# Rows of a mixture of experts: four quarter gathers and square-block transposes on VectorE in place of one gather and TensorE transposes

## The chip, the cores and the metric

The kernel runs on one core of one Trainium2 chip. The metric is the device time of one execution in microseconds (us); less is better. TensorE (PE) multiplies matrices into PSUM, VectorE (DVE), ScalarE (ACT) and GpSimd (POOL) work on elements, and SyncE (SP) and POOL issue the transfers (DMA) between HBM and SBUF. An engine takes its instructions in the order in which the program has them in that engine's queue.

## The reference, cut to what matters

One layer of a decoder for 512 prompt tokens, 64 sample tokens and 16 meta tokens of width 1024: attention and gated linear attention, and then a mixture of experts for the 576 tokens that are returned. Only the last part is touched:

```python
def hier_moe(h, w_group, b_group, w_er, b_er, w_g, w_u, w_d):
    hf = h.reshape(n * l, d)                       # RMSNorm of the residual stream, d = 1024
    ...                                            # top-1 group of 4, then top-2 of its 8 experts
    gates = jnp.sum(jax.nn.one_hot(e_id, N_EXPERTS, dtype=F32) * w_sel[..., None], axis=1)
    y = jnp.zeros_like(hf)
    for e in range(N_EXPERTS):                     # 32
        he = jax.nn.silu(hf @ w_g[e]) * (hf @ w_u[e])   # 1024 -> 256, twice
        y = y + gates[:, e:e + 1] * (he @ w_d[e])       # 256 -> 1024
    return y.reshape(n, l, d)
```

## The kernel before, in words

The last third of the program is the mixture of experts. `out_proj` ends the mixer; while its last quarter of columns is multiplied, `route_tile(i)` runs for each of five tiles of 128 tokens. It transposes the residual rows, computes the router's logits, scales the rows and writes them to `h2d` in HBM (L1217, L1218), and finds each token's two experts and its place among that expert's tokens. `table_tile` adds the tile to a table: a comparison on DVE (`pc`, L1278) and a product on PE (L1281) per choice. `tables` then makes from it, for 16 pairs of experts with 64 slots each, so 128 slots a pair, the row number `ix`, the token `tk` and the `gate` of each slot.

`moe` walks over the 16 pairs (`ep`). For a pair, `gather_x` fetches the 128 slots' rows into one of three tiles `xg` (an indirect DMA on POOL's queue, three pairs ahead), and `slots_t` turns them into `xt`, eight blocks of 128 features by 128 slots: eight transposes on PE into PSUM (L1340), then four copies by ACT and one by DVE that scale by `gk` (L1342, L1346). `pair_up` multiplies `xt` by the gate and up weights into `pj` (with the transposes of the pair before, `prod_t`, in its middle), ACT and DVE make `th` (L1359 to L1361). `pair_down` multiplies the pair before by its down weights into `dn`; ACT and DVE split the result into a high and a low half, `yh` (L1385) and `yl` (L1386). After every second pair `add_back` sends two pairs' results back to the tokens' rows: ten groups of four products `ab` on PE, each added to `x2` by DVE (L1400); two PSUM buffers hold the groups (`psA`).

In a round of the loop the order on every engine is the order of the code, since `mm`, `tr` and the marked DVE instructions are kept in program order: `pair_up(ep)`, `down(ep - 1)`, `slots_t` of pair ep + 1, and in every second round `back()`. Below, a round with `back()` is a long round (seven in the loop, plus the last `back` behind it), one without it a short round (pair ep + 1 prepared with no `ab` behind). The weights come through SP's queue into rings of buffers; those of experts 4 and 5 wait for small copies on POOL (L1309).

Of the kernel before, what the change touches and what calls it, by code (L numbers as in the profile page):

```python
# [11 lines left out]
F32 = mybir.dt.float32  # L12
F32R = mybir.dt.float32r
I32 = mybir.dt.int32
# [12 lines left out]
NQ = NP_ + NS  # L27
# [38 lines left out]
class Kern:  # L66
# [1086 lines left out]
    def route(self, rp):  # L1153
        nc, A, c = self.nc, self.A, self.rcp
        wr = rp.tile([128, 8, 36], F32, name="wr")
        nc.sync.dma_start(wr[:, :, 0:4], A["w_group_router"][0].rearrange("(k p) n -> p k n", p=128))
        nc.sync.dma_start(wr[:, :, 4:36], A["w_expert_router"][0].rearrange("(k p) n -> p k n", p=128))
        self.gk = c.tile([128, 8], F32, name="gk")
        nc.sync.dma_start(self.gk, A["norm_ffn_g"].rearrange("o (p k) -> p (o k)", p=128))
        gk = rp.tile([128, 8], F32, name="gkr")  # L1160
        nc.sync.dma_start(gk, A["norm_ffn_g"].rearrange("o (k p) -> p (o k)", p=128), allow_slow_non_contiguous=True)
        nc.gpsimd.tensor_tensor(wr, wr, gk[:, :, None].to_broadcast([128, 8, 36]), op=OP.mult)
        br = rp.tile([128, 36], F32, name="br")
        nc.sync.dma_start(br[:, 0:4], A["b_group_router"].to_broadcast([128, 4]))
        nc.sync.dma_start(br[:, 4:36], A["b_expert_router"].to_broadcast([128, 32]))
        self.i640 = c.tile([128, 640], F32, name="i640")
        nc.gpsimd.iota(self.i640, pattern=[[1, 640]], base=0, channel_multiplier=0, allow_small_or_imprecise_dtypes=True)
        i64 = c.tile([128, 64], F32, name="i64")
        nc.gpsimd.iota(i64, pattern=[[1, 64]], base=0, channel_multiplier=0, allow_small_or_imprecise_dtypes=True)
        tri = rp.tile([128, 128], BF16, name="tri")  # L1170
        ob = rp.tile([128, 128], BF16, name="ob")
        tf = rp.tile([128, 128], F32, name="trif")
        nc.gpsimd.memset(tf, 1.0)
        nc.gpsimd.affine_select(tf, tf, pattern=[[1, 128]], compare_op=OP.is_gt, fill=0.0, base=0, channel_multiplier=-1)
        nc.vector.tensor_copy(tri, tf)
        nc.vector.memset(ob, 1.0)
        iu = self.iu = rp.tile([128, 32], U32, name="iu")
        nc.vector.tensor_copy(iu, i64[:, 0:32])
        oh = c.tile([128, 5, 2, 32], BF16, name="oh")
        nc.gpsimd.memset(oh, 0.0)  # L1180

        val = c.tile([128, 5, 2, 2], F32, name="val")
        nc.gpsimd.memset(val[:, 4, :, 1], 0.0)
        for r in range(2):
            nc.gpsimd.iota(val[:, :, r, 0], pattern=[[128, 5]], base=-int(FAR), channel_multiplier=1, allow_small_or_imprecise_dtypes=True)
        pos = c.tile([128, 5, 2], F32, name="pos")
        self.oh, self.val, self.pos, self.i64 = oh, val, pos, i64
        self.rt = (rp, wr, br, tri, ob)
        self.tps = self.S2()[:, 0]

    def route_tile(self, i):
# [22 lines left out]
        lg = t(36, "lg")  # L1214
        nc.vector.scalar_tensor_tensor(lg[:w], ps[:w, 0:36], ss[:w], br[:w], op0=OP.mult, op1=OP.add)

        nc.scalar.activation(h2[:w].rearrange("t (k p) -> t p k", k=8), x.rearrange("t (p k) -> t p k", k=8), AF.Copy, scale=ss[:w])  # L1217
        nc.sync.dma_start(self.h2d[i * 128:i * 128 + w, :], h2[:w])  # L1218
        g8 = t(8, "g8")
        nc.gpsimd.memset(g8, NEG)  # L1220
# [52 lines left out]
    def table_tile(self, tp, ps, i):  # L1273

        nc = self.nc
        for r in range(2):
            pc = tp.tile([128, 2, 64], F32, name="pc", bufs=2)
            nc.vector.tensor_scalar(pc, self.i64[:, None, :].to_broadcast([128, 2, 64]), self.pos[:, i, r:r + 1], None, op0=OP.is_equal)  # L1278
            ov = tp.tile([128, 2, 32], F32, name="ov", bufs=2)
            nc.gpsimd.tensor_tensor(ov, self.oh[:, i, r, None, :].to_broadcast([128, 2, 32]), self.val[:, i, r, :, None].to_broadcast([128, 2, 32]), op=OP.mult)  # L1280
            nc.tensor.matmul(ps[:, 0:64], lhsT=pc.rearrange("p a b -> p (a b)"), rhs=ov.rearrange("p a b -> p (a b)"),  # L1281
                             start=(i == 0 and r == 0), stop=(i == 4 and r == 1))

    def tables(self, tp, c, ps):

        nc = self.nc
        psv = ps[:, 0:64].rearrange("p (a b e) -> p a b e", a=2, e=2)
        ix = c.tile([128, 16], I32, name="ix")
        tk = c.tile([128, 16], F32, name="tk")
        gate = c.tile([128, 16], F32, name="gate")  # L1290
        hs = [slice(64 * e, 64 * e + 64) for e in range(2)]
        for e, q in enumerate(hs):
            nc.vector.tensor_scalar(ix[q], psv[q, 0, :, e], FAR, None, op0=OP.add)
        for e, q in enumerate(hs):
            nc.vector.tensor_scalar(tk[q], psv[q, 0, :, e], FAR, None, op0=OP.add)
            nc.vector.tensor_scalar(gate[q], psv[q, 1, :, e], 0.5, None, op0=OP.mult)
        return tk, gate, ix


    def gather_x(self, xg, col):  # L1300
        self.nc.gpsimd.indirect_dma_start(xg, None, self.h2d[:, :], bass.IndirectOffsetOnAxis(ap=col, axis=0),  # L1301
                                          bounds_check=NQ - 1, oob_is_err=False)

    def load_up(self, pool, e, behind=None):

# [27 lines left out]
    def slots_t(self, xg, mp):  # L1333

        nc = self.nc
        xt = mp.tile([128, 8, 128], F32, name="xt")
        for q in range(2):
            ps = self.tp_()
            for k in range(4):
                self.tr(ps[:, k * 128:(k + 1) * 128], xg[:, (4 * q + k) * 128:(4 * q + k + 1) * 128], self.ident)  # L1340
            if q:
                nc.vector.tensor_tensor(xt[:, 4:8], ps.rearrange("p (k t) -> p k t", t=128),  # L1342
                                        self.gk[:, 4:8, None].to_broadcast([128, 4, 128]), op=OP.mult)
            else:
                for k in range(4):
                    nc.scalar.activation(xt[:, k], ps[:, k * 128:k * 128 + 128], AF.Copy, scale=self.gk[:, k:k + 1])  # L1346
        return xt

    def pair_up(self, xt, ws, mp, step=None):
# [54 lines left out]
    def moe(self, mp, gp, wxs):  # L1404
# [6 lines left out]
        def gather(ep):  # L1411
            if ep < 16:
                G[ep] = xgs[ep % 3]
                if ep < 3:
                    nc.gpsimd.memset(G[ep], 0.0)
                self.gather_x(G[ep], ix[:, ep:ep + 1])
        def up(e, **kw):
            if e < 32:
                U[e] = self.load(self.load_up(wxs[0].next(), slice(e, e + 1), kw.pop("behind", None)), **kw)
# [49 lines left out]
    def overflow(self):  # L1469

        nc, A, tc = self.nc, self.A, self.tc
        with tc.If(self.cnt > self.cap):
            with self.pool("ow", 2, side="right") as ow, self.pool("om", 1, side="right") as om:
                tab = self.drp.tile([3, 16, 128], F32, name="tab")
                with tc.For_i(0, (NQ + 63) // 64 - 1, 1):
                    nc.vector.tensor_scalar(self.pos, self.pos, 64.0, None, op0=OP.subtract)
                    ps = self.tp_()
                    for i in range(5):
                        self.table_tile(om, ps, i)
                    tk, gate, ix = self.tables(om, om, ps)  # L1480
                    for j, t in enumerate((ix.bitcast(F32), tk, gate)):
                        nc.sync.dma_start(tab[j].rearrange("e p -> p e"), t, allow_slow_non_contiguous=True)
                    with tc.For_i(0, 16, 1) as ep:
                        es = [bass.ds(ep * 2 + e2, 1) for e2 in range(2)]
                        up = [self.load(self.load_up(ow, e)) for e in es]
                        down = [self.load(self.load_down(ow, e)) for e in es]
                        col = om.tile([128, 3], F32, name="ocol")
                        for j in range(3):
                            nc.sync.dma_start(col[:, j:j + 1], tab[j, bass.ds(ep, 1)].rearrange("o p -> p o"))
                        xg = om.tile([128, D], F32, name="oxg")  # L1490
                        nc.gpsimd.memset(xg, 0.0)
                        self.gather_x(xg, col[:, 0:1].bitcast(I32))
                        hT = self.prod_t(self.pair_up(self.slots_t(xg, om), up, om), om)
                        self.add_back([self.pair_down(hT, down, col[:, 2:3], col[:, 1:2], om)])
            with self.pool("fin2", 1) as fp:
                for i in range(5):
                    for _ in self.final(fp.tile([128, D], F32, name="fo"), fp, i):
                        pass
# [184 lines left out]
```

## Time and profile before

| | |
|---|---|
| median of 3 runs | 1002.77 us (999.01 to 1008.5) |
| the profiled execution | 1004.81 us, its span 1003.1 us |
| PE busy in the span | 902.7 us (90%) |
| DVE, ACT, POOL busy | 496.3, 288.1, 236.8 us |
| mean granted PE clock | 0.954 of full speed |
| mixture of experts, from the first gather | 708.9 us to the end of the span |

Times in the profile count from the start of the span. A row of the chain of waits is start, length and what the last-ended work was at that time; the granted clock is 1.00 at 2.4 GHz and 0.50 at 1.2 GHz.

### The profile page before, as it was taken

To read this page: it belongs to the slowest core of one execution; us is meant where nothing else is said; L and a number is where in the kernel's file an instruction comes from. 1 tells how busy PE (TensorE), PEld (TensorE's weight loads), DVE (VectorE), ACT (ScalarE), POOL (GpSimd) and SP (SyncE) were. 2 spreads that over 40 slices of the span, in tenths; PEclk is the share of its full clock that TensorE was granted. 3 is DMA by queue.
4 is the path that set the end of the run, shared out by engine and by line. 5 is a ranking of instruction groups with operands and counts; after the bars stand their busy time and mean duration, and the time that the engine had idled before them with its cause. 6 is when DMAs were issued, how large, how long until landed. Compare 5 with 4: busy or idle time off the path is not lost. (4 is left out here: it accounts for less than half of the span.)

```text
span 1003.1 us, 18937 instructions
## 1 busy us (share of the span) xinstructions
PE 902.7 (90%) x7768; PEld 692.8 (69%) x7768; DVE 496.3 (49%) x1122; ACT 288.1 (29%) x647; POOL 236.8 (24%) x364
## 2 busy tenths in 40 slices
PE   3989989989699799998599998999799999999994
PEld 3878868678598699887598898998344453445342
DVE  5633545457465577645575156326423442444245
ACT  4114444332224214232333233116221122112112
POOL 5221101224245414233521244213300000000001
PEclk9989988999799899999799999999699999999997
DMA  7242322177469687798998766922899999999522
GB/s 206 61 124 67 87 77 67 54 248 241 132 221 305 240 304 229 243 334 281 327 392 283 252 195 182 311 100 99 329 416 413 391 412 379 377 407 392 211 84 96
DMA packets 123887, 239.97 MB, mean 239 GB/s; under 512 B 15084, under 2 KB 88700, under 8 KB 107412
## 3 DMA queue, kind: packets, MB, share of 16 engines
q1 hardware_dynamic: 107268, 160.78, 46.2%
q0 software_dynamic: 11664, 72.36, 19.2%
q10 hardware_dynamic: 4864, 5.57, 1.7%
q8 instruction: 62, 1.02, 0.4%
q14 instruction: 29, 0.24, 0.1%
HBM read 226.53 MB, written 15.83 MB: 242 GB/s over the span
## 5 line engine op out<-in xcount | busy, mean ns | idle before, releaser
L138 PE MATMUL pj<-hth,wh 128*128 128x288 f32 (+2 forms) x656 | 208.9, 318 | 1.8 <-DVE kt L381 1.8
L138 PE MATMUL pj<-htl,wh 128*128 128x288 f32 (+2 forms) x656 | 201.6, 307 | 0.0
L138 PE MATMUL pj<-hth,wl 128*128 128x288 f32 (+2 forms) x656 | 201.3, 307 | 0.0
L138 PEld LDWEIGHTS pj<-hth,wh 128*128 128x128 f32 (+1 forms) x656 | 128.3, 196 | 11.6 <-issue 7.1
L138 PEld LDWEIGHTS pj<-htl,wh 128*128 128x128 f32 (+1 forms) x656 | 128.1, 195 | 1.4 <-issue 0.8
L138 PEld LDWEIGHTS pj<-hth,wl 128*128 128x128 f32 (+1 forms) x656 | 127.6, 194 | 1.3 <-issue 0.2
L1328 PE MATMUL pj<-wgu,xt 128*64 128x512 f32 x512 | 119.4, 607 | 0.6
L1328 PEld LDWEIGHTS pj<-wgu,xt 128*64 128x64 f32 x512 | 38.7, 139 | 61.6 <-issue 56.9
L125 DVE TENSOR_TENSOR wl<-w,wh 128x1024 fp32r<-128x1024 f32 (+1 forms) x41 | 52.0, 1269 | 54.6 <-ACT wh L123 54.6
L1017 DVE STREAM_TRANSPOSE K<-K 128x2048 f32<-128x2048 f32 x32 | 73.6, 2303 | 7.8 <-DMA K<-in_cache_k_dram,idx 5.0
L123 ACT ACTIVATE wh<-w 128x1024 fp32r<-128x1024 f32 (+2 forms) x57 | 52.6, 924 | 60.0 <-PE pj L138 55.1
L1328 PE MATMUL ab<-yh,S 128*128 128x512 f32 (+1 forms) x160 | 66.7, 417 | 1.0 <-DVE x L1400 0.9
L1400 DVE TENSOR_TENSOR x<-x,ab 128x512 f32<-128x512 f32 (+1 forms) x80 | 54.5, 684 | 17.3 <-PE ab L1328 17.3
L1328 PE MATMUL ab<-yl,S 128*128 128x512 f32 (+1 forms) x160 | 63.0, 394 | 0.0
L1360 DVE SCALAR_TENSOR_TENSOR th<-th,pj 128x256 f32<-128x256 f32 x16 | 6.7, 421 | 113.0 <-ACT th L1359 104.0
L1301 POOL DMA_INDIRECT xg<-h2d,ix x16 | 16.1, 1007 | 182.9 <-PE tp L1331 180.8
L1328 PE MATMUL dn<-wdn,heT 128*64 128x512 f32 x256 | 57.7, 592 | 0.7 <-ACT heT L1369 0.7
L892 POOL DMA_INDIRECT V<-in_cache_v_dram,idx x32 | 31.7, 992 | 61.5 <-PE tp L988 42.0
L1328 PEld LDWEIGHTS dn<-wdn,heT 128*64 128x64 f32 x256 | 18.4, 137 | 36.8 <-issue 35.9
L1328 PEld LDWEIGHTS ab<-yh,S 128*128 128x128 f32 (+1 forms) x160 | 28.3, 177 | 21.6 <-DVE x L1400 15.2
L892 POOL DMA_INDIRECT K<-in_cache_k_dram,idx x32 | 32.4, 1013 | 40.0 <-PE S L925 19.9
L1386 DVE SCALAR_TENSOR_TENSOR yl<-dn,gate,yh 128x512 fp32r<-128x512 f32 x32 | 24.0, 751 | 35.0 <-ACT yh L1385 35.0
(424 smaller groups left out, 1605.5 us busy)
## 6 DMA issues: line engine op xcount, KB each, us to landing
wdn<-in_w_expert_down_dram SPq DMA_DIRECT2D x32, 1024.0 KB
wgu<-in_w_expert_gate_dram SPq DMA_DIRECT2D x32, 1024.0 KB
wgu<-in_w_expert_up_dram SPq DMA_DIRECT2D x32, 1024.0 KB
w<-in_w_in_dram SPq DMA_DIRECT2D x40, 512.0 KB
gtd<-sm ACTq DMA_DIRECT2D x32, 144.0 KB
gt<-gtd SPq DMA_DIRECT2D x8, 576.0 KB
R<-rdr SPq DMA_DIRECT2D x16, 256.0 KB
w<-in_w_o_dram SPq DMA_DIRECT2D x8, 512.0 KB
```

The source lines that it names most:

```text
L123: keep(nc.scalar.activation(hi, raw, AF.Copy))
L125: keep(e.tensor_tensor(lo, raw, hi.bitcast(F32), op=OP.subtract))
L138: nc.tensor.matmul(ps, lhsT=w[:, kt, :], rhs=r[:, kt, cs], start=(kt == 0 and j == 0), stop=(kt == nk - 1 and j == 2))
L892: nc.gpsimd.indirect_dma_start(t, None, view, bass.IndirectOffsetOnAxis(ap=self.idx[:, which, i:i + 1], axis=0)))
L1017: self.tc.keep_in_program_order(nc.vector.transpose(t, t))
L1301: self.nc.gpsimd.indirect_dma_start(xg, None, self.h2d[:, :], bass.IndirectOffsetOnAxis(ap=col, axis=0), bounds_check=NQ - 1, oob_is_err=F ...
L1328: self.tc.keep_in_program_order(self.nc.tensor.matmul(*a, **kw))
L1360: nc.vector.scalar_tensor_tensor(th, th, 1.0, gu[:, 0:256], op0=OP.add, op1=OP.mult)
L1386: nc.vector.scalar_tensor_tensor(yl[:, nh], dn, gate, yh[:, nh].bitcast(F32), op0=OP.mult, op1=OP.subtract)
L1400: self.tc.keep_in_program_order(nc.vector.tensor_tensor(x, x, ps[:w], op=OP.add))
```

## The change

The row of a slot is fetched in four quarters of 256 features. The table gets a second form: for each block `b` of 32 slots, partition p of `ix[:, b]` holds 4 x token + p // 32 for slot 32 b + p % 32. Four indirect DMAs a pair then place quarter p // 32 of that slot's row in columns 256 b to 256 b + 255 of partition p, so that a transposition of each 32 by 32 square in place, one DVE instruction (L1356), leaves features on partitions and slots in the columns. One DVE product with `gk` (L1357) writes `xt` in its old layout. PE's eight transposes a pair and the five scaled copies are gone; `route_tile` writes `h2d` in a layout that fits, and `table_tile` has one more comparison (`pq`) and two more products per choice. The part for experts with over 64 tokens is changed alike.

```diff
+        self.qoff = c.tile([128, 1], F32, name="qoff")
+        nc.vector.tensor_copy(self.qoff, qi[:, 1:2])
+        nc.vector.tensor_scalar(self.qoff, self.qoff, 4 * FAR, None, op0=OP.add)
...
-        nc.scalar.activation(h2[:w].rearrange("t (k p) -> t p k", k=8), x.rearrange("t (p k) -> t p k", k=8), AF.Copy, scale=ss[:w])
+        nc.scalar.activation(h2[:w].rearrange("t (q k p) -> t q p k", q=4, k=8), x.rearrange("t (q p k) -> t q p k", q=4, k=8), AF.Copy, scale=ss[:w])
...
+            pq = tp.tile([128, 2, 4, 32], F32, name="pq", bufs=2)
+            nc.vector.tensor_scalar(pq, self.i64.rearrange("p (h s) -> p h s", h=2)[:, :, None, :].to_broadcast([128, 2, 4, 32]),
+                                    self.pos[:, i, r:r + 1], None, op0=OP.is_equal)
+            for hb in range(2):
+                nc.tensor.matmul(ps[:, 64 + 32 * hb:96 + 32 * hb], lhsT=pq[:, hb].rearrange("p a b -> p (a b)"), rhs=ov[:, 0, :],
+                                 start=False, stop=(i == 4 and r == 1 and hb == 1))
...
-    def gather_x(self, xg, col):
-        self.nc.gpsimd.indirect_dma_start(xg, None, self.h2d[:, :], bass.IndirectOffsetOnAxis(ap=col, axis=0),
-                                          bounds_check=NQ - 1, oob_is_err=False)
+    def gather_x(self, xg, cols):
+
+        for b in range(4):
+            self.nc.gpsimd.indirect_dma_start(xg[:, b * 256:(b + 1) * 256], None, self.h2d.rearrange("t (q f) -> (t q) f", q=4),
+                                              bass.IndirectOffsetOnAxis(ap=cols[b], axis=0), bounds_check=4 * NQ - 1, oob_is_err=False)
...
-        for q in range(2):
-            ps = self.tp_()
-            for k in range(4):
-                self.tr(ps[:, k * 128:(k + 1) * 128], xg[:, (4 * q + k) * 128:(4 * q + k + 1) * 128], self.ident)
-            if q:
-                nc.vector.tensor_tensor(xt[:, 4:8], ps.rearrange("p (k t) -> p k t", t=128),
-                                        self.gk[:, 4:8, None].to_broadcast([128, 4, 128]), op=OP.mult)
-            else:
-                for k in range(4):
-                    nc.scalar.activation(xt[:, k], ps[:, k * 128:k * 128 + 128], AF.Copy, scale=self.gk[:, k:k + 1])
+        self.tc.keep_in_program_order(nc.vector.transpose(xg, xg))
+        nc.vector.tensor_tensor(xt.rearrange("p c (b j) -> p b c j", b=4), xg.rearrange("p (b c j) -> p b c j", b=4, c=8),
+                                self.gk[:, None, :, None].to_broadcast([128, 4, 8, 32]), op=OP.mult)
...
-                self.gather_x(G[ep], ix[:, ep:ep + 1])
+                self.gather_x(G[ep], [ix[:, b, ep:ep + 1] for b in range(4)])
```

DVE's queue through a short and a long round, before (a row is line, operation, what is written from what, shape; `x` is the residual `x2`):

```order
L1360 SCALAR_TENSOR_TENSOR th<-th,pj 128x256
L1361 TENSOR_TENSOR th<-th,pj 128x256
L1386 SCALAR_TENSOR_TENSOR yl<-dn,gate,yh 128x512 x2
L1342 TENSOR_TENSOR xt<-tp,gk 128x512
L1360 SCALAR_TENSOR_TENSOR th<-th,pj 128x256
L1361 TENSOR_TENSOR th<-th,pj 128x256
L1386 SCALAR_TENSOR_TENSOR yl<-dn,gate,yh 128x512 x2
L1342 TENSOR_TENSOR xt<-tp,gk 128x512
L1400 TENSOR_TENSOR x_6498<-x_6498,ab 128x512 x8
```

The same stretch of DVE's queue in the changed kernel:

```order
L1372 SCALAR_TENSOR_TENSOR th<-th,pj 128x256
L1373 TENSOR_TENSOR th<-th,pj 128x256
L1398 SCALAR_TENSOR_TENSOR yl<-dn,gate,yh 128x512 x2
L1356 STREAM_TRANSPOSE xg_8237<-xg_8237 128x1024
L1357 TENSOR_TENSOR xt<-xg_8237,gk 128x4x8x32
L1372 SCALAR_TENSOR_TENSOR th<-th,pj 128x256
L1373 TENSOR_TENSOR th<-th,pj 128x256
L1398 SCALAR_TENSOR_TENSOR yl<-dn,gate,yh 128x512 x2
L1356 STREAM_TRANSPOSE xg_8235<-xg_8235 128x1024
L1357 TENSOR_TENSOR xt<-xg_8235,gk 128x4x8x32
L1412 TENSOR_TENSOR x_6498<-x_6498,ab 128x512 x8
```

In both rounds the transposition and the product now stand where one half-sized copy stood: behind both `yl`, and in the long round ahead of the additions.

POOL's queue from the first gather on, before (the `wgu` copies are those for which the loads of experts 4 and 5 wait):

```order
L1301 DMA xg_8189<-h2d,ix 128x1024
L1415 MEMSET xg_8190 128x1024
L1415 MEMSET xg_8191 128x1024
L1301 DMA xg_8190<-h2d,ix 128x1024
L1309 COPY wgu<-tk 1x1 x2
L1301 DMA xg_8191<-h2d,ix 128x1024
L1309 COPY wgu<-tk 1x1 x2
```

POOL's queue from the first gather on, in the changed kernel:

```order
L1320 DMA xg_8235<-h2d,ix 128x256 x4
L1427 MEMSET xg_8236 128x1024
L1427 MEMSET xg_8237 128x1024
L1320 DMA xg_8236<-h2d,ix 128x256 x4
L1328 COPY wgu<-tk 1x1 x2
L1320 DMA xg_8237<-h2d,ix 128x256 x4
L1328 COPY wgu<-tk 1x1 x2
```

Each gather is four instructions in place of one, and the first copies stand behind eight gather instructions in place of two.

## Rows read from the trace of the kernel before

**Rows 1.** The page: busy time of each engine, share of the span, instructions.

```profile
PE 902.7 (90%) x7768; PEld 692.8 (69%) x7768; DVE 496.3 (49%) x1122; ACT 288.1 (29%) x647; POOL 236.8 (24%) x364
```

**Rows 2.** Chain of waits, a short and a long round: start us, us, what.

```profile
767.00 3.48 PE dn L1328 x16
...
770.51 0.56 ACT yh L1385
...
771.53 3.72 PE pj L1328 x16
...
782.64 1.02 PE tp L1331 x8
783.66 9.79 PE ab L1328 x40
793.45 3.58 PE pj L1328 x16
```

**Rows 3.** Timeline, end of `dn` and start of `ab` in that long round.

```profile
782.72 0.69 ACT L1385 ACTIVATE yh<-dn,gate 128x512 fp32r<-128x512 f32 x1 [1.06 <-PE dn L1328]
...
783.44 0.75 DVE L1386 SCALAR_TENSOR_TENSOR yl<-dn,gate,yh 128x512 fp32r<-128x512 f32 x1 [0.99 <-ACT yh L1385]
...
784.10 0.68 DVE L1342 TENSOR_TENSOR xt<-tp,gk 128x512 f32<-128x512 f32 x1
...
784.70 0.68 DVE L1400 TENSOR_TENSOR x<-x,ab 128x512 f32<-128x512 f32 x1
...
785.43 0.19 PEld L1328 LDWEIGHTS ab<-yh,S 128*128 128x128 f32 x1 [0.34 <-DVE x L1400]
```

**Rows 4.** Groups by line, DVE's transpositions: shapes, count | busy us, mean ns | idle before.

```profile
L1017 DVE STREAM_TRANSPOSE K<-K 128x2048 f32<-128x2048 f32 x32 | 73.6, 2303 | 7.8 <-DMA K<-in_cache_k_dram,idx 5.0 <-issue 2.6
L876 DVE STREAM_TRANSPOSE oga<-M 128x32 f32<-128x32 f32 x16 | 3.4, 210 | 0.4
```

**Rows 5.** Groups by line from 600 us to 716 us, columns as in group 4.

```profile
L1217 ACT ACTIVATE h<-x,rss 128x1024 f32<-128x1024 f32 x4 | 8.3, 2083 | 2.3 <-POOL rss L1210 2.3
...
L125 DVE TENSOR_TENSOR wgu<-w,wgu 128x1024 fp32r<-128x1024 f32 x4 | 4.9, 1225 | 3.3 <-ACT wgu L123 3.3
...
L1376 DVE TENSOR_SCALAR S<-i,tk 128x640 fp32r<-128x640 f32 x2 | 3.5, 1804 | 0.0
...
L1278 DVE TENSOR_SCALAR pc<-i,pos 128x128 f32<-128x128 f32 x10 | 2.7, 312 | 0.1
```

**Rows 6.** Stretches: length, busy us of five engines, granted PE clock, DMA share, GB/s.

```profile
623.00:629.00 6.00, 4.08 (x32) 4.06 (x32) 5.40 (x8) 2.43 (x3) 2.71 (x6) 1.00 1.07 243
219.90:223.60 3.70, 0.02 (x2) 0.00 (x0) 3.70 (x5) 0.71 (x3) 0.00 (x0) 1.00 0.98 316
224.50:227.80 3.30, 3.30 (x23) 2.96 (x13) 1.21 (x1) 0.00 (x0) 0.94 (x1) 0.50 0.72 204
556.60:559.00 2.40, 0.00 (x1) 0.00 (x0) 1.23 (x1) 0.90 (x1) 0.00 (x0) 0.99 0.33 123
559.10:562.30 3.20, 3.20 (x38) 2.72 (x39) 0.00 (x0) 0.28 (x1) 0.00 (x0) 0.50 0.63 125
713.10:719.30 6.20, 6.16 (x18) 2.82 (x20) 0.69 (x1) 1.14 (x4) 2.68 (x7) 0.50 0.87 329
```

**Rows 7.** Chain of waits, from the last table product to the first pair.

```profile
707.12 1.10 PE S L1281 x4
...
708.89 4.11 DMA xg<-h2d,ix
...
715.09 9.16 PE pj L1328 x32
```

**Rows 8.** View of line 1301, the gathers on POOL.

```profile
L1301 POOL DMA_INDIRECT xg<-h2d,ix x16: 988/990/1156, 708.9 to 907.6; - x16
...
DMA to landing us min/median/max: 8.2/8.6/9.1
```

**Rows 9.** Stretches again, in the router's part.

```profile
680.00:690.00 10.00, 9.70 (x87) 9.20 (x87) 6.84 (x33) 7.31 (x14) 3.48 (x12) 1.00 0.19 73
```

More of the change, by code (lines that the diff above doesn't have):

```diff
@@ L1186, in route @@
         pos = c.tile([128, 5, 2], F32, name="pos")
+        qi = rp.tile([128, 2], I32, name="qi")
+        nc.gpsimd.iota(qi[:, 0:1], pattern=[[0, 1]], base=0, channel_multiplier=1)
+        nc.vector.tensor_scalar(qi[:, 1:2], qi[:, 0:1], 5, None, op0=OP.logical_shift_right)
+        self.qoff = c.tile([128, 1], F32, name="qoff")
+        nc.vector.tensor_copy(self.qoff, qi[:, 1:2])
+        nc.vector.tensor_scalar(self.qoff, self.qoff, 4 * FAR, None, op0=OP.add)
         self.oh, self.val, self.pos, self.i64 = oh, val, pos, i64
@@ L1281, in table_tile @@
             nc.tensor.matmul(ps[:, 0:64], lhsT=pc.rearrange("p a b -> p (a b)"), rhs=ov.rearrange("p a b -> p (a b)"),
-                             start=(i == 0 and r == 0), stop=(i == 4 and r == 1))
+                             start=(i == 0 and r == 0), stop=False)
+            pq = tp.tile([128, 2, 4, 32], F32, name="pq", bufs=2)
[4 more added lines that the diff above has]
+                                 start=False, stop=(i == 4 and r == 1 and hb == 1))
     def tables(self, tp, c, ps):
@@ L1287, in tables @@
         psv = ps[:, 0:64].rearrange("p (a b e) -> p a b e", a=2, e=2)
-        ix = c.tile([128, 16], I32, name="ix")
+        ix = c.tile([128, 4, 16], I32, name="ix")
         tk = c.tile([128, 16], F32, name="tk")
@@ L1291, in tables @@
         hs = [slice(64 * e, 64 * e + 64) for e in range(2)]
-        for e, q in enumerate(hs):
-            nc.vector.tensor_scalar(ix[q], psv[q, 0, :, e], FAR, None, op0=OP.add)
+        for e in range(2):
+            nc.vector.tensor_scalar(ix[:, 2 * e:2 * e + 2], ps[:, 64:128].rearrange("p (h b e) -> p h b e", h=2, e=2)[:, :, :, e], 4.0, self.qoff,
+                                    op0=OP.mult, op1=OP.add)
         for e, q in enumerate(hs):
@@ L1473, in overflow @@
             with self.pool("ow", 2, side="right") as ow, self.pool("om", 1, side="right") as om:
-                tab = self.drp.tile([3, 16, 128], F32, name="tab")
+                tab = self.drp.tile([6, 16, 128], F32, name="tab")
                 with tc.For_i(0, (NQ + 63) // 64 - 1, 1):
@@ L1480, in overflow @@
                     tk, gate, ix = self.tables(om, om, ps)
-                    for j, t in enumerate((ix.bitcast(F32), tk, gate)):
+                    for j, t in enumerate([ix[:, b].bitcast(F32) for b in range(4)] + [tk, gate]):
                         nc.sync.dma_start(tab[j].rearrange("e p -> p e"), t, allow_slow_non_contiguous=True)
@@ L1486, in overflow @@
                         down = [self.load(self.load_down(ow, e)) for e in es]
-                        col = om.tile([128, 3], F32, name="ocol")
-                        for j in range(3):
+                        col = om.tile([128, 6], F32, name="ocol")
+                        for j in range(6):
                             nc.sync.dma_start(col[:, j:j + 1], tab[j, bass.ds(ep, 1)].rearrange("o p -> p o"))
@@ L1491, in overflow @@
                         nc.gpsimd.memset(xg, 0.0)
-                        self.gather_x(xg, col[:, 0:1].bitcast(I32))
+                        self.gather_x(xg, [col[:, b:b + 1].bitcast(I32) for b in range(4)])
                         hT = self.prod_t(self.pair_up(self.slots_t(xg, om), up, om), om)
-                        self.add_back([self.pair_down(hT, down, col[:, 2:3], col[:, 1:2], om)])
+                        self.add_back([self.pair_down(hT, down, col[:, 5:6], col[:, 4:5], om)])
             with self.pool("fin2", 1) as fp:
```

## The prediction

> **What bounds the kernel now.** I read the page's busy times first, then the chain of waits through the mixture of experts, then the timeline of one long round, and last the granted clock beside PE's idle stretches. PE is busy for 902.7 of 1003.1 us [rows 1], and the chain shows it without a gap from `dn` to `pj` to `ab`; so a round is as long as PE's queue, and what is put between two of PE's products is paid in full. In a short round `dn` (3.48 us) ends, ACT makes the second `yh`, then the first scaled block of `xt`, and `pj` starts 1.02 us after that `yh` did (771.53 - 770.51) [rows 2]; PE's eight transposes run inside that second. In a long round the eight transposes take 1.02 us of the chain, `ab` 9.79 us, and the next `pj` follows at once, with `xt` long done [rows 2]. DVE is half idle [rows 1], but what matters is its place in the row: both `yl` end after PE's last `dn`, and DVE reaches `xt` only then [rows 3].
>
> **Removed.** Eight transposes a pair (1.02 us of PE, [rows 2]), four copies of ACT and one of 0.68 us on DVE [rows 3].
>
> **Added on DVE, twice 16 instructions.** The trace has square-block transposes of 128x2048 at 2.303 us and of 128x32 at 0.210 us [rows 4]; on a line between them 128x1024 takes 1.24 us (1.15 if it is half of the large one). The product with `gk`, SBUF to SBUF, is nearest to the 128x1024 product of L125 at 1.225 us [rows 5], which I take; since it writes in pieces of 32 columns, the upper bound is the scattered copy of L1217 at 2.083 us [rows 5], though that is ACT's. The order of DVE's queue has both behind `yl` in every round.
>
> *Short rounds.* From the start of the second `yh` to that of its `yl` are 0.72 us, and from there to DVE's next instruction 0.66 us [rows 3]. Then 1.24 + 0.04 (a handoff, as between two dependent instructions elsewhere in the chain, an estimate) + 1.22 + 0.04: `pj` starts 3.92 us after `yh`, where it is now 1.02. That is 2.90 us more, less 0.14 since `pj` no longer waits for ACT's blocks one by one (3.72 against 3.58 [rows 2]): 2.76 us. Seven short rounds prepare pairs 2, 4, ... 14; pair 1 behind the first `pj` has `th` in the place of `yl` and costs the same. **8 x 2.76 = 22 us.** PE is idle for some 3.9 us each time.
>
> *Long rounds.* `ab` now follows `dn` at once, but only two groups have a buffer. The third needs the first addition, which stood behind 0.60 us of `xt` (784.10 to 784.70) [rows 3] and now stands behind transposition and product: 784.10 + 1.24 + 0.04 + 1.22 - 0.08 (independent instructions of DVE start that much before the end of the one ahead, 784.78 against 784.70) = 786.52, done at 787.20, so that the third group starts at 787.25 and not at 785.43 [rows 3]. From there the additions keep up as before. **7 x 1.82 = 13 us.** The 1.02 us that PE saves are in it: it gets to the wait sooner, and is idle for some 2.6 us in each (two groups are 1.96 us of the 9.79 behind `dn`).
>
> The Trainium skill (VectorE: DVE Perf Modes, The three transpose paths) gives a 128x128 bf16 block 311 ns on VectorE against 390 ns on TensorE, by which the move itself would gain. Our rows put it the other way for a pair's eight blocks, an estimated 1.24 us against 1.02 us; at eight times the page's 311 ns, 2.49 us, the sum would be 15 x 1.25 = 19 us higher (an estimate from that page).
>
> **What the stalls do to PE's clock.** In the trace an idle stretch of 3.7 us (219.9 to 223.6) is followed by 3.3 us at half clock with PE at work all the time, and one of 2.4 us (556.6 to 559.0) by 3.2 us at half clock; one of 1.9 us (the idle part of 623.0 to 629.0) kept the full clock [rows 6]. So I expect all eight stalls of 3.9 us to be followed by such a stretch, and half of the seven of 2.6 us, since they lie just above the shortest that did it: 11 or 12 of 15. Half clock for 3.3 us loses 1.65 us of a dense row of products; I take 1.5, since a part falls into the stall. **11.5 x 1.5 = 17 us**, between 0 (the clock holds) and 15 x 1.65 = 25.
>
> **The router.** Two comparisons `pq` of 128x256 a tile: above `pc`'s 0.31 us [rows 5], say 0.35, so 0.7 us of DVE a tile. Four more products a tile, each two pieces: four pieces took 1.10 us at half clock [rows 7], so eight at full clock about 1.1 us. Four tiles run where PE is 97% busy [rows 9]; up to 4 us there, of which DVE's part mostly runs beside PE. The last tile is alone: 0.7 us of DVE, up to 2 us of PE. I take **4 us** (1 to 6). The new writing order of `h2` goes at the scattered rate that it has already [rows 5]: 0, at most 1 us if ACT's copy got faster or slower by half.
>
> **The start.** The first gather is on the path: 4.11 us from issue to landing [rows 7], with one instruction of POOL at 0.99 us [rows 8]; three more put the landing 3.0 us later, less if a quarter lands sooner. From landing (713.0) to `pj` (715.09) were 2.1 us [rows 7], now 1.24 + 1.22 + three handoffs = 2.6. And PE, which got half clock until 719.3 [rows 6], so for 4.2 us of `pj`, begins cold with `pj` itself: for up to 6.2 us, 1 us more lost. **4.5 us** in all (2 to 9: the upper end has the quarters land one behind the other, and DVE's first product held by POOL, as the two `S` beside POOL's fills were, at 1.80 us mean and 3.5 us together [rows 5]).
>
> Costed at nothing: *Gathers later on.* POOL spends 4 us on one instead of 1, but is idle for three quarters of the time [rows 1], and each is issued three pairs ahead, at least 41 us (three times 3.58 + 3.58 + 3.48, and one `ab` of 9.79 [rows 2]); even four landings of 8.6 us [rows 8] in a row are 34 us. *Experts 4 and 5.* Their copies on POOL stand behind six more gather instructions, so SP's queue, in order, issues their loads 6 to 9 us later; but pair 2 starts some 12 us later too, counted from the first gather, by the terms here. If that cover fails, it costs 2 to 5 us once. *ACT* loses work; its `yh` waits for nothing new.
>
> **Sum.** 22 + 13 + 17 + 4 + 4.5 = 60.5 us. The profiled execution took 1004.81 us, 2.0 above the median of the runs, so 1065.3 by it and **1063 us** as a median.
>
> **Rivals.** *The clock holds* through stalls of this length inside a dense stretch: the sum without 17 us, 1046 us. For it: only two rows of idling in dense work were followed by a fall. Against: both were shorter than the eight long stalls. *Slow writes*: the product with `gk` takes 2.08 us; 15 x 0.86 = 13 us more, and the longer stalls of the long rounds all bring the clock down, 4 x 1.5 = 6 us: 1082 us. For it L1217; against it, DVE's copies with `gk` from PSUM into the same tile run at the rate of its additions (0.68 us both, [rows 3]). *The other side: DVE gets its transposition done under PE's work.* The rows are landed long before; if transposition and product ran while DVE waits for `th` in a round, `xt` would be ready when `dn` ends. Then each short round loses its 1.02 + 0.14 us and each long round the 1.02 us of transposes: 8 x 1.16 + 7 x 1.02 = 16 us less, and with router and start 1004.8 - 16 + 8.5 - 2 = 995 us, 0.8% faster. It decides at one point: whether the transposition stands ahead of `yl` in DVE's queue. It stands behind in each of the rounds, so this needs an engine that works out of order. *Hidden anyway*: stalls on PE are covered by the weights' transfers being late; but no transfer of weights ends a wait of PE in the chain, and slower rounds only give the transfers room.
>
> **How the numbers follow.** The forecast has a chance of 0.75, the clock that holds 0.10, slow writes or gathers 0.08, the faster case 0.02, other mishaps 0.05. The range is 1044 to 1079 us: below, the first rival with the low ends of start and router (1046 - 2); above, the sum with 25 us of clock, 6 and 9 us for router and start (1077), and 2 us for durations. The slow-write case and the faster one are left out. A difference of 1% is about what a measurement of this kernel can tell from none. Faster by over 1%: 0.01; within 1%: 0.03, from the faster case and from stalls that half vanish; slower by over 1%: 0.96.
>
> **What would show it.** In the changed profile: 16 square-block transposes of about 1.24 us and 16 products of about 1.22 us; PE waiting for the product (L1357) some eight times for 3.9 us before `pj`, and seven times for an addition (L1412) for 2.6 us inside `ab`; a short and a long round together some 7 us longer than before; half clock in ten to fifteen short stretches after 720 us; first `pj` at 722 to 725 us with the router's delay in it. The prediction is wrong if `pj` follows `dn` without that wait, if the clock stays at 1.00 behind the stalls, or if PE waits for a gather or for weights.

## The result and the profile after

The changed kernel takes 1068.08 us (median of 4 runs, 1063.14 to 1070.22), beside 1004.53 us for the kernel before on the same chip: a ratio of 1.065 (95% interval 1.061 to 1.069), so slower by some 64 us. The profiled execution took 1070.22 us, its span is 1068.4 us. The forecast was 1063 us in a range of 1044 to 1079.

The page's busy times, and the view of groups by line for the lines that the change added (busy us, mean ns | idle before):

```profile
PE 920.5 (86%) x7680; PEld 702.1 (66%) x7680; DVE 523.8 (49%) x1151; ACT 271.4 (25%) x583; POOL 286.8 (27%) x413
...
L1320 POOL DMA_INDIRECT xg<-h2d,ix x64 | 65.2, 1019 | 189.7 <-DVE xt L1357 157.6 <-issue 15.1 <-DVE x L1412 13.4
...
L1356 DVE STREAM_TRANSPOSE xg<-xg 128x1024 f32<-128x1024 f32 x16 | 19.8, 1235 | 5.2 <-DMA xg<-h2d,ix 5.2
L1357 DVE TENSOR_TENSOR xt<-xg,gk 128x1024 f32<-128x1024 f32 x16 | 19.6, 1225 | 0.6
```

PE has 88 instructions fewer than in [rows 1] and is busy 17.8 us longer. Its work did not grow: part of it ran at half clock. The two new instructions on DVE take 1.235 and 1.225 us, as forecast (1.24 and 1.22), and DVE is still idle half of the time.

The chain of waits through a long and a short round, in the place of [rows 2]:

```profile
803.29 3.48 PE dn L1347 x16
...
806.80 0.70 ACT yh L1397
...
808.18 1.25 DVE xg L1356
...
809.46 1.23 DVE xt L1357
810.68 0.61 DVE x L1412
...
811.34 9.52 PE ab L1347 x32
820.86 3.58 PE pj L1347 x16
...
828.39 3.48 PE dn L1347 x16
...
831.90 0.69 ACT yh L1397
...
833.29 1.25 DVE xg L1356
...
834.56 1.24 DVE xt L1357
...
835.84 5.02 PE pj L1347 x16
```

In the short round `pj` starts 3.94 us after the second `yh` (835.84 - 831.90), where it was 1.02 in [rows 2], and those 16 products then take 5.02 us (5.42 in most short rounds) where others take 3.58. In the long round `ab` (eight of its forty products lie ahead of the wait, so the row has 32) has to wait for an addition that now stands behind transposition and product, as the timeline of DVE there shows in the place of [rows 3]:

```profile
807.52 0.75 DVE L1398 SCALAR_TENSOR_TENSOR yl<-dn,gate,yh 128x512 fp32r<-128x512 f32 x1 [0.99 <-ACT yh L1397]
808.18 1.24 DVE L1356 STREAM_TRANSPOSE xg<-xg 128x1024 f32<-128x1024 f32 x1
809.46 1.23 DVE L1357 TENSOR_TENSOR xt<-xg,gk 128x1024 f32<-128x1024 f32 x1
810.60 1.28 DVE L1412 TENSOR_TENSOR x<-x,ab 128x512 f32<-128x512 f32 x2
```

PE's waits from 725 us to the end (us in total, times, longest):

```profile
PE pj L1347 <- DVE xt L1357: 27.9, 7, 4.0
PE ab L1347 <- DVE x L1412: 18.5, 9, 2.5
PE pj L1347 <- issue: 4.2, 1, 4.2
```

Seven waits of 4.0 us before `pj` and an eighth of 4.2 us, put down to "issue", are the eight short rounds. Of the nine waits inside `ab`, two belong to the last `back` (0.9 us in the kernel before, where they stand alone), which leaves seven of 2.5 us. Together that is some 50 us in which PE does nothing.

The view of stretches shows what the clock does around them (columns as in [rows 6]: length, busy us of PE, PEld, DVE, ACT and POOL with counts, granted clock):

```profile
736.20:739.60 3.40, 3.40 (x11) 1.51 (x9) 0.00 (x0) 0.00 (x0) 2.77 (x3) 0.50 1.02 405
...
806.80:811.30 4.50, 2.03 (x8) 1.27 (x8) 3.75 (x5) 0.69 (x1) 0.35 (x1) 0.99 1.01 422
811.30:814.70 3.40, 3.37 (x8) 2.69 (x9) 1.27 (x2) 0.00 (x0) 2.64 (x3) 0.50 1.02 429
```

Each stretch at 0.50 (1.2 GHz) begins near the end of a wait: from 0.7 us before PE takes up work (835.1 against 835.84, which is why `pj` took 5.02 us there) to 1.1 us after it (736.2 against 735.10). In four of the stretches 0.3 to 0.8 us fall into the wait; in the others PE is busy throughout. From 730 us to the end of the loop there are 15, one at each of the 15 waits, two of them twice as long (6.9 us); the kernel before has none between 719 us and the end of its loop.

The chain at the start of the experts, in the place of [rows 7]:

```profile
709.46 0.35 DVE pc L1285
...
713.27 0.31 POOL xg L1320
...
714.74 1.00 POOL xg L1320
...
716.04 1.00 POOL xg L1320
...
717.34 2.48 DMA xg<-h2d,ix
...
722.50 8.82 PE pj L1347 x32
```

From the last tile's first `pc` to the first gather's issue are 3.81 us here and were 2.26 before (706.63 to 708.89), since four products of `pq` stand between those of `pc`. From that issue to the landing are 6.6 us in place of 4.11: three more gathers, 1.3 us apart on POOL, less what the last small one lands sooner. And from landing to `pj` 2.65 in place of 2.1.

### The profile page after: what moved, and what is told of

Same layout as the page of the kernel before. It is cut to its first block, busy times and chain, and to the rows that moved or that the text cites. A ratio compares the mean times of both kernels' runs of the same rounds, so it can differ in the third digit from the quotient of the medians.

```text
span 1068.4 us, 18836 instructions
## 1 busy us (share of the span) xinstructions
PE 920.5 (86%) x7680; PEld 702.1 (66%) x7680; DVE 523.8 (49%) x1151; ACT 271.4 (25%) x583; POOL 286.8 (27%) x413
## 3 DMA queue, kind: packets, MB, share of 16 engines
q8 instruction: 62, 1.02, 0.4%
## 5 line engine op out<-in xcount | busy, mean ns | idle before, releaser
L1347 PE MATMUL pj<-wgu,xt 128*64 128x512 f32 x512 | 133.4, 667 | 41.8 <-DVE xt L1357 37.7
L1347 PEld LDWEIGHTS pj<-wgu,xt 128*64 128x64 f32 x512 | 44.2, 151 | 116.0 <-issue 71.5
L1320 POOL DMA_INDIRECT xg<-h2d,ix x64 | 65.2, 1019 | 189.7 <-DVE xt L1357 157.6
L1347 PE MATMUL ab<-yh,S 128*128 128x512 f32 (+1 forms) x160 | 73.8, 462 | 18.6 <-DVE x L1412 18.5
L1347 PE MATMUL ab<-yl,S 128*128 128x512 f32 (+1 forms) x160 | 70.3, 439 | 0.0
L1347 PEld LDWEIGHTS ab<-yh,S 128*128 128x128 f32 (+1 forms) x160 | 32.9, 205 | 43.7 <-DVE x L1412 29.5
L1381 ACT ACTIVATE heT<-tp 128x256 f32<-128x256 f32 x16 | 6.1, 383 | 196.9 <-PE tp L1350 187.7
L892 POOL DMA_INDIRECT K<-in_cache_k_dram,idx x32 | 33.1, 1035 | 36.7 <-PE S L925 20.6
```

The costliest lines, as they stand in the source:

```text
L892: nc.gpsimd.indirect_dma_start(t, None, view, bass.IndirectOffsetOnAxis(ap=self.idx[:, which, i:i + 1], axis=0)))
L1320: self.nc.gpsimd.indirect_dma_start(xg[:, b * 256:(b + 1) * 256], None, self.h2d.rearrange("t (q f) -> (t q) f", q=4), bass.IndirectOffset ...
L1347: self.tc.keep_in_program_order(self.nc.tensor.matmul(*a, **kw))
```

## The experiments

All ratios are to the kernel before, run beside them on the same chip; 1% is 10 us. The changed kernel stands at 1.065.

**1. The same two instructions, ahead in DVE's queue.** `slots_t` for the next pair is called behind the first k-step of `pair_up`, so that DVE has it done before `th` and `yl` are due.

```diff
...
             def step(k):
+                if k == 0 and ep < 15:
+                    X[ep + 1] = self.slots_t(G[ep + 1], mp)
                 if k == 3 and ep:
...
-            if ep < 15:
-                xt = self.slots_t(G[ep + 1], mp)
...
```

> The changed kernel with one move: transposition and product for pair ep + 1 are issued behind the first block of pair ep's products, so in DVE's queue they stand ahead of th and yl; the instructions are the same. Theory (the cost is their place in DVE's queue): the stalls and the half clock behind them go, PE keeps the saving of its transposes, about 996 us (988 to 1004). Rival (the DVE work itself, four-part gathers or contention cost the time wherever they stand): 1045 us or more.

Measured: 1001.23 us, ratio 0.998 (0.994 to 1.002). The whole loss is gone. In its chain of waits `pj` follows `dn` without a gap and at full clock, and the next long round shows what is late instead:

```profile
770.75 3.43 PE dn L1347 x16
774.18 3.43 PE pj L1347 x16
...
781.57 3.48 PE dn L1347 x16
...
785.07 0.70 ACT yh L1397
...
785.79 0.75 DVE yl L1398
786.54 0.61 DVE x L1412
...
787.19 8.01 PE ab L1347 x32
```

The second `yl` and the first addition now hold the third group of `ab`; the 1.02 us of transposes had covered a part of that.

Two kernels with one half of the change each follow. Their layout of rows and their transposition don't fit each other, so the parts of rows are mixed up in both; the amount of work is that of the full kernels.

**2. The quarters alone**: the changed kernel's layout of `h2d`, its table and its four gathers, with the eight transposes on PE and the five copies as before.

```diff
-        self.tc.keep_in_program_order(nc.vector.transpose(xg, xg))
-        nc.vector.tensor_tensor(xt.rearrange("p c (b j) -> p b c j", b=4), xg.rearrange("p (b c j) -> p b c j", b=4, c=8),
-                                self.gk[:, None, :, None].to_broadcast([128, 4, 8, 32]), op=OP.mult)
+        for q in range(2):
+            ps = self.tp_()
+            for k in range(4):
+                self.tr(ps[:, k * 128:(k + 1) * 128], xg[:, (4 * q + k) * 128:(4 * q + k + 1) * 128], self.ident)
...
```

> Quarter gathers, the longer table and the new layout of h2 as in the changed kernel, but PE's eight transposes and the scaled copies of the kernel before (features and slots are mixed up by it, so the experts get other numbers). Theory: only router and start cost anything, about 1012 us (1008 to 1017). Rival (quarter gathers are late or take bandwidth in every pair): 1025 us or more.

Measured: 1016.78 us, ratio 1.011 (1.007 to 1.015): 11 us, where 8.5 were forecast for router and start. Its trace shows that they do not all lie there. From the router's first logits to the first `pj` are 8.1 us more than before, and the loop behind, up to the last `yh`, is 7.3 us longer. PE waits 5.8 us of that in one piece for `heT`, at a time when ACT stood still for something that the profile puts to none of the program's engines and queues, as the chain of waits and the page show:

```profile
733.64 12.27 another core or an unknown queue
```

```profile
L1347 PE MATMUL dn<-wdn,heT 128*64 128x512 f32 x256 | 59.7, 609 | 6.5 <-ACT heT L1388 6.5
```

Behind the last `yh` 3.6 us less pass than before.

**3. The transposition alone**: the kernel before with its table and its one gather, and in `slots_t` the transposition and the product of the changed kernel (the edit above the other way round).

> The kernel before, one gather a pair and the old table, with only the transposes of PE replaced by DVE's transposition and product at the same place in the code (features and slots are mixed up by it, so the experts get other numbers). Theory: nearly the whole loss, 1058 us (1052 to 1065). Rival (half of the loss is in gathers, table and start): 1035 us or less.

Measured: 1065.5 us, ratio 1.061 (1.057 to 1.064), with 15 stretches at half clock as in the changed kernel. So almost all of the loss comes with the two DVE instructions and, by run 1, from their place; it is some 9 us more than the 52 us that the forecast has for stalls and clock.

**4. TensorE kept busy in the stalls.** Products with a zero matrix into `pj`'s own sum stand where PE would wait: eight in a short round, and five inside `ab` in a long one.

```diff
+    def zeros(self, n):
+        for j in range(n):
+            self.mm(self.gu[0:64], lhsT=self.z64, rhs=self.i640[:, 0:512], start=(j == 0), stop=False)
...
+                self.gu = self.pj_()
+                if len(done) < 2:
+                    self.zeros(8)
```

> The changed kernel with products by a tile of zeros added to the next pair's sum while PE waits: eight in each short round, five in each long one, short enough to end before the wait does. The stalls stay, PE is not idle in them. Theory (the clock falls because PE idles, and that is 17 to 25 us of the loss): the clock stays at 1.00 from 735 us on and the time is about 1046 us (1040 to 1053). Rival (the stalls alone make the loss, the clock changes nothing): 1068 us, as the changed kernel.

Measured: 1073.43 us, ratio 1.069 (1.065 to 1.074): neither number. The chain tells why. Eight zero products and 16 of `pj` took 10.29 us in one row, and 10.29 - 3.43 = 6.86 us for eight is 0.86 us each, 0.43 us for each of its two pieces. These products fill only one expert's 64 rows of `pj`; where the two experts' products stand in turn, a piece takes 0.22 us on the mean (3.58 over 16). The filling was longer than the gap by 2.9 us in a short round and 2 us in a long one, some 37 us in all. Yet the clock stayed at 1.00 from 725 to 1060 us, so this run spoke for the clock's part without giving its price. Hence the next.

**5. The same with four and two zero products** (3.4 us for a wait of 4.0, 1.7 us for one of 2.4).

> The changed kernel with zero products (which add nothing to the sums) filling TensorE's stalls, sized this time from the earlier run: a zero product took 0.86 us (two pieces of 0.43), so four (3.4 us) go into a short round's wait of 4.0 us and two (1.7 us) into a long round's wait of 2.4 us. Theory (about 25 us of the loss is the clock: 15 stretches at half clock, about 1.84 us each in short rounds and 1.5 us in long ones): the granted clock stays at 1.00 after the start and the time is 1068.1 - 15 - 11 = 1043 us (1038 to 1050). Rival (the low clock is not what costs; the products wait for something else that is late anyhow): 1068 us (1064 to 1072) with or without a steady clock. If the clock still falls with a gap of under 1 us left, then 1060 to 1070.

Measured: 1039.65 us, ratio 1.042 (1.038 to 1.047). Stretches and chain:

```profile
725.00:1030.00 305.00, 292.39 (x1186) 121.89 (x1182) 136.55 (x192) 41.00 (x84) 57.67 (x64) 1.00 0.77 305
```

```profile
782.65 1.24 DVE xt L1357
...
783.93 3.72 PE pj L1347 x16
...
799.00 0.61 DVE x L1417
...
799.65 8.00 PE ab L1347 x32
```

`pj` waits for `xt` as long as before and starts 3.93 us after `yh` (780.00), but the 16 products after it take 3.72 us and not 5.42, and the 32 of `ab` 8.00 and not 9.5. Work that adds nothing made the kernel 22.6 us faster than the changed one (1.0646 - 1.0421 of 1003 us): that is the clock's share, with some 6 us either way by the two intervals.

**6. Ahead in the short rounds alone, and 7. in the long ones alone.** The edit of run 6 against run 1 (run 7 has `not` ahead of the bracket):

```diff
-                if k == 0 and ep < 15:
+                if k == 0 and ep < 15 and (ep == 0 or ep % 2 == 1):
...
+            if ep < 15 and ep + 1 not in X:
+                X[ep + 1] = self.slots_t(G[ep + 1], mp)
```

> The changed kernel with the transposition and the product taken ahead (issued after the first k-step of the round before) for the 8 short rounds alone; the 7 long rounds stay as in the changed kernel. Theory (each short round pays 2.76 us of stall and 1.84 us of half clock in the next products): 1068.1 - 8 x 4.6 = 1031 us (1025 to 1037), with half-clock stretches left only behind the long rounds' stalls (7 of them). Rival: the long rounds' stall of 2.4 us alone does not make the clock fall, so that their 7 x 1.5 us go as well: 1021 us (1016 to 1025) and no low stretch. Second rival: the loss is not made in the short rounds: 1050 us or more.

> The changed kernel with the transposition and the product taken ahead for the 7 long rounds alone; the 8 short rounds stay as in the changed kernel. Theory (each long round pays 1.82 us of stall and 1.5 us of half clock in the add-back's products): 1068.1 - 7 x 3.3 = 1045 us (1039 to 1051), with 8 half-clock stretches left. Rival: the long rounds lose less when moved, since yl's second half then holds the add-back up by 0.75 us: 1050 us; second rival: nothing is lost in long rounds, 1066 us or more. The gains of the short and the long rounds alone should add up to that of both together (1068.1 - 1001.2 = 67 us)  if no state is shared between them; theory says 37 + 23 = 60.

Measured: short rounds 1013.63 us, ratio 1.015 (1.010 to 1.019), so 50 us less than the changed kernel; long rounds 1037.47 us, 1.040 (1.036 to 1.044), so 25 us less. The kernel before took 997.8 us beside these two, so times are not those of the expectations and the gains are compared: 37 were expected for the short rounds and 23 for the long ones. The first was too small for a plain reason: moving the work ahead takes away the whole wait of 4.0 us, not just the 2.76 us by which it is longer than before; 8 x (4.0 + 1.84) is 47 us. With the short rounds' waits gone, the long ones still bring the clock down, all seven of them:

```profile
783.70:788.20 4.50, 2.02 (x8) 1.28 (x8) 3.74 (x5) 0.69 (x1) 0.34 (x1) 0.99 1.00 411
788.20:791.60 3.40, 3.36 (x8) 2.69 (x9) 1.27 (x2) 0.00 (x0) 2.66 (x3) 0.52 1.03 411
```

PE idles 2.5 of 4.5 us there, and its next products are at half clock; so the rival of run 6, that the long waits alone leave the clock up, falls. Both gains add up to 75 us, where run 1 gained 67; the intervals (4 to 5 us for each) cover the difference.

**8. The cheap table.** Run 1 still pays for the quarters. Here the wide comparison and its products go; four products with a constant 0/1 matrix replicate the finished token numbers.

```diff
-            pq = tp.tile([128, 2, 4, 32], F32, name="pq", bufs=2)
...
+        rs = self.tp_()
+        for b in range(4):
+            nc.tensor.matmul(rs[:, 16 * b:16 * b + 16], lhsT=self.rep[:, b].rearrange("p a j -> p (a j)"), rhs=tk, start=(b == 0), stop=(b == 3))
+        nc.vector.tensor_scalar(ix, rs[:, 0:64].rearrange("p (b e) -> p b e", b=4), 4.0, self.qoff, op0=OP.mult, op1=OP.add)
...
```

> The kernel with transposition and product ahead in all rounds (1001.2 us before), and in addition the quarters' table is built without the wider comparison and two more products in each of the router's ten steps: the finished table of token numbers is replicated by four products with a constant 0/1 matrix. Theory (the wider table costs 4.4 us over the router's five tiles and about 0.9 us more between the last comparison and the first gather's issue, all on the path): 1001.2 - 5.3 = 996 us (992 to 999), ratio to the kernel before 0.993 (0.990 to 0.997). Rival (that time on the path is given back by a later wait, for instance weights that land at their own time): 1001 us (1000 to 1003). The four gathers of the first pair stay, about 2.4 us more than before.

Measured: 993.49 us beside 997.78 us, ratio 0.997 (0.994 to 0.999), which overlaps with run 1's. So both were timed again together, with two more that part the 11 us of run 2 and price the change without quarters.

**9 to 12.**

> The transposition and product taken ahead in all rounds, timed again beside the kernel with the cheap table. Earlier ratio 0.998 (0.994 to 1.002); a table that costs about 5 us on the path should leave it 0.3 to 0.6% above the cheap-table kernel; if the weights' arrival takes that back, they are within 0.2% of each other.

> The kernel with the cheap table, timed again beside the one without: 0.997 (0.994 to 0.999) of the kernel before by the earlier run, and 0.995 if the table's 5 us are all on the path.

> Quarters gathered in four, transposed by TensorE as in the kernel before (its numbers are then mixed up among the rows), with the cheap table: this parts the 11 us that the quarters with the wide table cost into table and gathers. Theory (by the traces: the router's five tiles +4.4 to 5.4 us and about 0.9 us at the table's end go, about 1.0 us of table end and 2.4 us of four gathers in a row before the first products stay): ratio 1.005 (1.002 to 1.008), some 5 to 6 us less than with the wide table. Rival (the gathers, which hold GpSimd for 1.3 us each ahead of the late weights' issue, are the price): 1.009 to 1.012.

> The old table and one gather per pair (so the transposed squares hold the wrong rows' parts, and the output is not the reference's), with the transposition and product by DVE taken ahead in all rounds: what the change could bring if the quarters were free. Theory (two rounds take 32.0 us in place of 34.0: 7.5 x 2 = 15 us; start and router as before): 1003 - 15 = 988 us, ratio 0.985 (0.982 to 0.990). Rival (the weights' arrival sets the pace from there on, as two waits for weights of 3.8 us in all in the cheap-table kernel's trace hint): 0.990 to 0.996.

| run | ratio | interval |
|---|---|---|
| 9, ahead (again) | 0.997 | 0.994 to 0.999 |
| 10, ahead, cheap table (again) | 0.993 | 0.991 to 0.996 |
| 11, quarters with the cheap table, transposes on PE | 1.006 | 1.003 to 1.009 |
| 12, ahead, old table and one gather | 0.987 | 0.983 to 0.991 |

The cheap table takes 5 us off run 2 (1.011 to 1.006), as expected, though the two intervals meet. The quarters with it still cost 6 us, and the move itself, rightly placed, is worth 13 us. These add up: 0.987 + 0.006 = 0.993, which is run 10, and 0.987 + 0.011 = 0.998, which is run 1. The kernel with the cheap table beats both kernels, the one before by 0.3% (run 8) and 0.7% (run 10). From run 9 to run 10 the fall is 3 us by the medians of ratios and not 5, and the intervals meet. In run 10's trace, as in run 8's, PE waits for something that it waits for in no other, the down weights (waits from 725 to 970 us), while the transfers run at 0.99 of their engines' time; run 12, whose loop started sooner, shows no such wait:

```profile
PE dn L1342 <- DMA wdn<-in_w_expert_down_dram: 3.2, 2, 1.9
```

```profile
725.00:955.00 230.00, 225.81 (x979) 95.11 (x976) 116.44 (x164) 30.40 (x57) 58.30 (x58) 1.00 0.99 397
```

```profile
720.00:950.00 230.00, 229.32 (x1011) 97.19 (x1008) 119.47 (x170) 30.43 (x58) 10.87 (x11) 1.00 0.96 387
```

The last line is run 12's. The gathers keep POOL busy for 47 us more in run 10, and copies on POOL stand ahead of the loads of experts 4 and 5; whether these or the faster pace bring the wait was not tried apart.

The profiled executions show where the quarters cost time. From the router's first logits to the first `pj` pass 36.7 to 38.0 us with the old table and one gather, 44 to 46 us with the wide table, and 40 to 42 us with the cheap one. The loop, from the first `pj` to the last `yh`, takes 264.0 us in the kernel before, 271.3 and 270.1 in runs 2 and 11; with the work ahead it takes 248.5 us in run 12, and 255.7 to 255.9 in runs 1, 8, 9 and 10. So 6 to 7 us of the quarters' price lie inside the loop wherever its rounds are fast, and none where they are slow: 325.5 us in the changed kernel, 325.7 in run 3 without quarters. What comes late differs from trace to trace: the down weights in runs 8 and 10, and in runs 1, 2, 9 and 11 ACT, which stands still for 6 to 12 us in all for something unknown. Behind the last `yh` are 20.4 to 20.7 us with the quarters and 24.0 to 24.1 without. What causes the parts in the loop and behind it is open.

## Why the prediction was right, and where a term was off

The sum was 60.5 us; the two profiled spans differ by 65.3. The mechanism is the one forecast: waits of PE for DVE's queue, and half clock at the end of each. (The range's lower end takes 2 us off for the low ends of router and start; by the low ends stated, 1 and 2, it is 5.5 us, so some 1040 in place of 1044. Nothing hangs on it.) Term by term:

- **Short rounds, 8 x 2.76 = 22 us: right.** Both durations (1.235 and 1.225 us) and the start of `pj` 3.94 us after `yh` (3.92 forecast) are as worked out, and the wait is paid in full: run 1, which moves only its place, gets it back. Run 6 gains more than this term, since it removes the whole wait and not just its growth.
- **Long rounds, 7 x 1.82 = 13 us: right.** `ab` waits 2.5 us for the addition (2.6 forecast). By run 7's 25 us, wait and half clock together, the price of this place is shown.
- **The clock, 11.5 x 1.5 = 17 us: too small.** The step that failed is "half of the seven": all 15 waits brought the clock down, the long rounds' too. "Since a part falls into the stall" came true in four stretches only, and two stretches were twice as long, for which the sum had no term. Half clock cost 5.42 - 3.58 = 1.84 us in six short rounds (1.44 and 3.10 in the other two, where `pj` took 5.02 and 6.68) and 1.4 to 1.9 us in six long ones (9.4 to 9.9 against 8.0; 2.7 in the seventh). That is some 27 us, above the term's upper end of 25; run 5 measures 22.6 us, some 6 either way, with the waits left in place.
- **The router, 4 us, and the start, 4.5 us: right in sum, divided otherwise.** From the first tile's logits to the last tile's, 25.18 us grew to 29.6 (676.76 to 706.36): 4.4 us; the table's end adds 1.55 us, gathers 2.5 and transposition and product 0.5. That is 9 us in place of 8.5. Run 2's 11 us (7 to 15) are not this term alone, as its trace shows. The extra microsecond for PE starting cold was not there: `pj` got half clock for 3.4 us (722.5 to 725.9) where it had been 4.2.
- **A term that the sum did not have.** The loop grew from 264.0 to 325.5 us, by 61.5, for which the terms above give 22 + 13 + 27 = 62. With 9 us for router and start that is some 70 us, 5 more than the spans differ by. 1.6 us of these lie ahead of the change's part: this execution reached the router's first logits that much earlier. The other 3.6 us are saved behind the last `yh` (1047.97, before 979.05), where 20.4 us are left in place of 24.1. This comes with the quarters, since runs 3 and 12, without them, have 24.1 and 24.0; which part of them saves it is open.
- **Costed at nothing** holds for the changed kernel: PE waits neither for later gathers nor for weights. In runs 8 and 10, with faster rounds, the weights do come late, and with the quarters every fast loop is 6 to 7 us longer; the slow rounds of the changed kernel hide that.
- **The rivals.** *The clock holds* is refuted by the 15 stretches, and *slow writes* by 1.225 us for the product in pieces of 32 columns. *The other side*, 995 us, named the right condition, the transposition ahead of `yl`, and was priced somewhat too low: written into the program, it gave ratios of 0.998 and 0.997 where 0.992 was forecast. The move is worth 13 us by run 12 where 16 were forecast (its loop is 15.4 us shorter), and the quarters cost 11 by run 2 where it was 8.5.

The Trainium skill's two figures (VectorE: DVE Perf Modes, The three transpose paths), by which a 128x128 bf16 block is cheaper on VectorE than on TensorE, decided nothing. For the eight fp32 blocks of a pair the measured order is the other way, DVE's 1.235 us against PE's 1.02 us, and the same two DVE instructions cost some 60 us in one place of the queue (run 3) and in another brought 13 (run 12).

## What to carry to other kernels

An instruction that goes from the busiest engine to an idle one is free only if the receiving queue reaches it before the result is due; look for what stands ahead of it there (here `yl`, behind the last product) and issue it where that engine last had nothing to do. Price a stall of TensorE at its length and what the clock takes behind it: here 2.5 to 4.0 us of waiting cost another 1.4 to 1.9 us in most cases and up to 3.1. And look at what feeds the new form: four gathers in place of one and a wider table, with what comes late in the loop beside them, ate most of the 13 us that the move was worth.

## What the hardware showed that was not expected

- Short waits in dense work bring the granted clock from 1.00 to 0.50 every time here: 15 of 15, at 2.5 us as at 4.0 us. The low stretch lasts 3.4 us, twice 6.9, and begins between 0.7 us before PE works again and 1.1 us after it. With zero products in the waits, the clock stayed at 1.00 from 725 us to the end of the loop.
- A square-block transposition of 128x1024 in place takes 1.235 us, and a product that writes 32-column pieces 1.225 us, the same as the contiguous one of [rows 5].
- A product with 64 rows of output and 512 columns took 0.43 us a piece in a row of zero products (run 4), against 0.22 us on the mean where the two experts' products stand in turn [rows 2].
- An indirect gather of quarter rows holds POOL for 1.02 us, where a gather of whole rows held it for 0.99 us [rows 8]: the instruction's price did not follow the size of the row.
